# Tiles of their own for the retention's two outputs, beside a shared pool of nine slots

## The chip, the cores and the metric

One core of a Trainium2 chip runs the whole program. It has a matrix engine (PE in the profile, with its weight loads shown apart as PEld), a vector engine (DVE), a scalar engine (ACT), a GpSimd engine (POOL) and a queue that issues most transfers (SP). Each engine takes its own instructions strictly in the order in which they were placed at build time and stops at one whose inputs or whose memory are not free yet. The metric is the device time of one execution in microseconds, lower is better; the median of three runs is given.

## The reference

Two decoder layers on a sequence of 512 positions with 1024 channels, all in float32. A layer has three token mixers that share one input projection, a gated sum of their outputs, and a gated MLP:

```python
for l in range(DEPTH):                        # 2
    h = rmsnorm(x, norm_mix_g[l])
    proj = h @ w_in[l]                        # split into the pieces below
    # differential attention: 4 heads of 2 x 64, v of 128, blocks of 128 queries
    a = softmax(q1 @ k1 + bias) - lam * softmax(q2 @ k2 + bias)
    o_da = rmsnorm(a @ v, da_subln_g[l]) * (1.0 - lam_init)
    # retention: 4 heads of 64, chunks of 128, with rotary embedding
    o_ret = rmsnorm(retention(rq, rk, rv), ret_norm_g[l]) * silu(r_g)
    o_sc = sc_b * causal_dwconv(sc_c * sc_x, sc_conv_w[l], sc_conv_b[l])
    gates = sigmoid(gate_pre + b_gate[l])     # 3 x 1024
    y = (gates[0] * (o_da @ w_branch_da[l]) + gates[1] * (o_ret @ w_branch_ret[l])
         + gates[2] * (o_sc @ w_branch_sc[l]))
    x = x + y @ w_out[l]
    h = rmsnorm(x, norm_ffn_g[l])
    g_ff, u_ff = split(h @ w_ffn_in[l])       # 2 x 2816
    x = x + (silu(causal_dwconv(g_ff, ...)) * u_ff) @ w_ffn_out[l]
```

## The kernel before, in words

**Arithmetic.** Every float32 matrix product is made of three products in a faster format. An operand is split into a rounded part `hi` (a cast on ACT, line 150, 166 or 169) and the rest `lo` (a subtraction on DVE, line 151, 167 or 170), and `mm3` (lines 159 to 161) adds hi·hi, hi·lo and lo·hi. Weights are loaded by SP (line 137) into two raw slots and split into a ring of three `hi` and three `lo` tiles. A split activation is a pair of 128x512 tiles, that is 4 KB on each of the 128 partitions.

**The shared pool "N".** `pairN` and `wide` hand out tiles of 4 KB per partition with the tag N, of which there are nine (`NN = 9`). In the mixers of one layer these tiles live there: the retention's values `rv` (two), its gate `sg`, its natural keys `knh` and `knl`, its transposed queries and keys `rT` (four), and its outputs `omr0` and `omr1`; the short convolution's outputs `oms0` and `oms1`; and for each attention head h the projected queries and keys `nath`, the values `vh`, the transposed pair `qh` and `kh`, and the output `omh`. Later `y` and the MLP's `act` tiles follow. A new tile takes the slot of one whose last reader is done; until then its first writer waits.

**Order of the work.** The program text weaves two streams (`weave`): the first is the chain of small steps of the retention and of the four attention heads, the second (`filler`) the large projections. `filler` runs head 0's projection (PSUM tiles `pnh0`), the short convolution's first half, head 1's, its second half, head 2's, five steps of the short convolution's branch (`side(2)`), head 3's projection, and then the rest of `side(2)` and `side(1)`, the retention's branch. A piece of a side is a gate projection of 24 products 128x512 (`ptg16` to `ptg23` for side 2, `ptg8` to `ptg15` for side 1), followed by a branch projection of 6 (`pb02` to `pb72` and `pb01` to `pb71`; the first digit is the column block, the second the branch). At build time a scheduler with a timing model of its own then places the instructions of all streams on each engine, and gives out the slots in the order in which its model sees them free. So the size of a pool decides not only waits but the order itself.

**Where a head's projection ends.** `natural` fills all four PSUM banks of the pool `pm` ("main") with one head, 128 positions each. `evacuate` (lines 430 to 435) empties a bank in five steps: `nat` (ACT, 432), a square in place (ACT, 433), the split of the values into `v` (ACT, 169 and DVE, 170) and a sum of the squares into `msqk` (DVE, 435). Only when the last of these is done may the next user of the bank, for head 3 `pb22`, write there.

**The attention of a head** (lines 529 to 539) runs four query blocks i: scores `pS0hi` and `pS1hi` on PE (487, 488), bias and minimum on DVE (492), exponential on ACT (493), a combination on DVE (501 to 504), transposes `pThi` on PE (511), a split into `aThi` (ACT 166, DVE 167), products with the values into `po0h` or `po2h` on PE (523, 524), and `oh` (ACT 525, DVE 526). At the end `oh` is scaled (544), transposed into `ptoh` (284) and split into `omh` (169, 170).

**Two memory regions that alternate.** The layer's mixers have a pool `mp` on the right side of SBUF, and the MLP a pool there too, one after the other, over the same addresses. By the shapes in the program `mp` holds 55 KB per partition and the MLP's 64 KB.

Of the kernel before, what the change touches and what calls it, by code (L numbers as in the profile page):

```python
# [12 lines left out]
F32R = mybir.dt.float32r  # L13
# [7 lines left out]
P = 128  # L21
D = 1024
S = 512
# [25 lines left out]
G_MIX, G_FFN, B_GATE, G_Q, G_K, G_SUB, G_RET = 0, 8, 16, 40, 41, 42, 43  # L49
# [4 lines left out]
def trunk(ctx, tc, xT, wr, wh, wt, wda, wret, wsc, wo, wf, w2, par, lamp, relb, onehot, mask, rope, gtab, out):  # L54
# [20 lines left out]
    def pairN(name):  # L75
        return tp.tile([P, 2, S], F32R, tag="N", name=name, bufs=NN)
# [42 lines left out]
    def main(name):  # L119
        return pm.tile([P, S], F32, tag="main", name=name)  # L120
# [42 lines left out]
    def split(src, hi, lo, g=None):  # L163

        if g is None:
            A.copy(hi, src)
            V.tensor_tensor(lo, src, hi.bitcast(F32), ALU.subtract)
        else:
            A.activation(hi, src, AF.Copy, scale=g)
            V.scalar_tensor_tensor(lo, src, g, hi.bitcast(F32), ALU.mult, ALU.subtract)  # L170
        return hi, lo

    def split2(src, t, g=None):
        n = src.shape[-1]
        return split(src, t[:, 0, :n], t[:, 1, :n], g)
# [12 lines left out]
    ps = pa.tile([P, S], F32, tag="aux", name="ps_warm")  # L188
# [82 lines left out]
    def rms_cols(sq, n, scale, name):  # L271

        ms = small(n, f"ms{name}")
        V.tensor_reduce(ms, sq, AX.X, ALU.add)
        V.tensor_scalar(ms, ms, scale, EPS, ALU.mult, ALU.add)
        f = small(n, f"f{name}")
        rsqrt(f, ms, n, name)
        return f

    def transposes(src, name):  # L280

        ps = aux(name)
        for st in range(ST):
            T.transpose(ps[:, st * P : (st + 1) * P], src(st), ident)
        return ps
# [13 lines left out]
    def mix(l, mp):  # L299
        pt = pars[l]  # L300
        L = f"L{l}"
# [147 lines left out]
        om = [None] * KT  # L449
# [109 lines left out]
        def retention(p):  # L559
# [4 lines left out]
            for c in (p, 2 + p):  # L564
                ps = transposes(lambda st: rr[st][:, c * P : (c + 1) * P], f"ptr{c}{L}")
# [70 lines left out]
            f = rms_cols(sqv, 8, 1.0 / 64, f"r{p}{L}")  # L636
# [6 lines left out]
            yield  # L643
            yield
            ps = transposes(lambda st: o[:, st * P : (st + 1) * P], f"ptor{p}{L}")
            om[4 + p] = split2(ps, pairN(f"omr{p}{L}"), pt[:, G_RET : G_RET + 1])
            yield


# [75 lines left out]

        rest = filler()
        weave(staggered([(4 * p, retention(p)) for p in range(2)] + [(6 + 8 * h, attention(h)) for h in range(H)]), rest)

        y = []
# [5 lines left out]
        for e in range(KT):  # L735
            w = weights(wo[l, e], f"o{L}{e}")
            ps = main(f"po{e}{L}")
# [237 lines left out]
```

## Time and profile before

| | us |
|---|---|
| median of 3 runs (lowest, highest) | 1548.77 (1547.65, 1552.67) |
| the profiled execution, its own time | 1550.88 |
| its span from the first to the last instruction | 1549.1 |
| PE busy, PEld busy | 1526.5, 1345.9 |
| DVE busy, ACT busy | 1101.2, 731.9 |
| mean granted TensorE clock | 0.993 |

The profiled execution took 1550.88 us, of which 1.8 lie outside the span. A row of the timeline gives start, duration, engine, line, operation and tiles; brackets at its end give idle time of the engine just before it and what ended that. Layer numbers and buffer numbers are left out of names, so `v3L` is head 3's value tile in either layer, once in the first half of the span and once in the second. Where a matmul starts before the one ahead of it is shown to end, the two overlap in the engine's pipeline: the spacing of starts, not the duration, is what a matmul costs.

### The profile page before, as it was taken

To read this page: it belongs to the slowest core of one execution; us is meant where nothing else is said; L and a number is where in the kernel's file an instruction comes from. 1 tells how busy PE (TensorE), PEld (TensorE's weight loads), DVE (VectorE), ACT (ScalarE), POOL (GpSimd) and SP (SyncE) were. 2 spreads that over 40 slices of the span, in tenths; PEclk is the share of its full clock that TensorE was granted. 3 is DMA by queue.
4 is the path that set the end of the run, shared out by engine and by line. 5 is a ranking of instruction groups with operands and counts; after the bars stand their busy time and mean duration, and the time that the engine had idled before them with its cause. 6 is when DMAs were issued, how large, how long until landed. Compare 5 with 4: busy or idle time off the path is not lost.

```text
span 1549.1 us, 21866 instructions
## 1 busy us (share of the span) xinstructions
PE 1526.5 (99%) x8510; PEld 1345.9 (87%) x8510; DVE 1101.2 (71%) x2040; ACT 731.9 (47%) x1304; POOL 14.1 (1%) x27
## 2 busy tenths in 40 slices
PE   9999989999999999999999999899999999999998
PEld 7899878888887999899789999688888879988997
DVE  7588776655569996597666887665546789957963
ACT  4456555433344564365425565453334446634641
POOL 1000000000000000000100000000000000000000
PEclk9999999999999999999999999899999999999999
DMA  5322222232221332331322222222323132224213
GB/s 188 116 103 63 88 74 84 85 98 96 98 88 55 142 110 69 136 137 55 129 82 92 72 89 72 68 81 90 102 76 123 68 110 110 92 84 165 96 45 106
DMA packets 43287, 148.54 MB, mean 96 GB/s; under 512 B 5703, under 2 KB 6102, under 8 KB 37552
## 3 DMA queue, kind: packets, MB, share of 16 engines
q1 hardware_dynamic: 41328, 143.37, 27.7%
q0 software_dynamic: 1856, 3.77, 0.7%
q8 instruction: 67, 1.10, 0.3%
q14 instruction: 36, 0.29, 0.1%
HBM read 145.01 MB, written 3.42 MB: 96 GB/s over the span
## 4 chain that ended last, share of the span: by engine, by line
PE 92%; DVE 3%; DMA 2%; ACT 2%; issue 1%; SPq 0%; ACTq 0%; DVEq 0%
PE pnrvgL L161 1%; PE pnrvgL L159 1%; PE pnrvgL L160 1%; PE pnrqkL L160 1%; PE pnrqkL L161 1%; PE pnrqkL L159 1%; PE pnh2L L161 1%; PE pnh2L L160 1%; PE pnh2L L159 1%; PE pnh1L L161 1%; PE pnh1L L160 1%; PE pnh1L L159 1%; PE pnh0L L160 1%; PE pnh0L L159 1%; PE pnh0L L161 1%
## 5 line engine op out<-in xcount | busy, mean ns | idle before, releaser
L150 ACT CAST hi_tL<-raw_tL 128x1024 fp32r<-128x1024 f32 x60 | 62.9, 1049 | 135.0 <-DMA raw_tL<-in_wt 18.3
L150 ACT CAST hi_w2L<-raw_w2L 128x640 fp32r<-128x640 f32 (+2 forms) x64 | 49.4, 781 | 97.8 <-DMA raw_w2L<-in_w 49.8
L151 DVE TENSOR_TENSOR lo_tL<-raw_tL,hi_tL 128x1024 fp32r<-128x1024 f32 x60 | 73.4, 1224 | 19.0 <-ACT hi_tL L150 18.8
L151 DVE TENSOR_TENSOR lo_w2L<-raw_w2L,hi_w2L 128x640 fp32r<-128x640 f32 (+2 forms) x64 | 56.2, 889 | 37.8 <-ACT hi_w2L L150 35.7
L150 ACT CAST hi_fbL<-raw_fL 128x1024 fp32r<-128x1024 f32 x34 | 35.7, 1051 | 26.2 <-PE p216L L160 11.7
L150 ACT CAST hi_oL<-raw_oL 128x1024 fp32r<-128x1024 f32 x16 | 16.9, 1054 | 58.1 <-issue 19.5
L151 DVE TENSOR_TENSOR lo_fbL<-raw_fL,hi_fbL 128x1024 fp32r<-128x1024 f32 x34 | 41.6, 1222 | 1.7 <-ACT hi_fbL L150 1.6
L150 ACT CAST hi_faL<-raw_fL 128x512 fp32r<-128x512 f32 x34 | 21.1, 622 | 30.9 <-DMA raw_fL<-in_wf 26.8
L151 DVE TENSOR_TENSOR lo_fuL<-raw_fL,hi_fuL 128x1024 fp32r<-128x1024 f32 x10 | 12.2, 1224 | 19.6 <-ACT hi_fuL L150 19.6
L150 ACT CAST hi_fuL<-raw_fL 128x1024 fp32r<-128x1024 f32 x10 | 10.5, 1051 | 31.2 <-PE pg0L L160 11.0
L151 DVE TENSOR_TENSOR lo_faL<-raw_fL,hi_faL 128x512 fp32r<-128x512 f32 x34 | 23.4, 689 | 0.3
L150 ACT CAST hi_nrvgL<-raw_nrvgL 128x1024 fp32r<-128x1024 f32 x8 | 8.4, 1051 | 31.5 <-PE pnrvgL L161 13.5
L150 ACT CAST hi_fgL<-raw_fL 128x1024 fp32r<-128x1024 f32 x10 | 10.5, 1054 | 24.1 <-issue 9.5
L151 DVE TENSOR_TENSOR lo_oL<-raw_oL,hi_oL 128x1024 fp32r<-128x1024 f32 x16 | 19.6, 1224 | 2.8 <-ACT hi_oL L150 2.8
L151 DVE TENSOR_TENSOR lo_nrvgL<-raw_nrvgL,hi_nrvgL 128x1024 fp32r<-128x1024 f32 x8 | 9.8, 1224 | 12.6 <-ACT hi_nrvgL L150 12.6
L151 DVE TENSOR_TENSOR lo_nh0L<-raw_nh0L,hi_nh0L 128x768 fp32r<-128x768 f32 x8 | 7.7, 958 | 13.4 <-ACT hi_nh0L L150 13.4
L150 ACT CAST hi_nrqkL<-raw_nrqkL 128x1024 fp32r<-128x1024 f32 (+1 forms) x9 | 8.6, 953 | 16.1 <-issue 11.1
L150 ACT CAST hi_bdL<-raw_bdL 128x512 fp32r<-128x512 f32 x16 | 9.9, 618 | 10.7 <-PE pb50L L160 2.2
L151 DVE TENSOR_TENSOR lo_nrqkL<-raw_nrqkL,hi_nrqkL 128x1024 fp32r<-128x1024 f32 (+1 forms) x9 | 9.9, 1105 | 7.0 <-ACT hi_nrqkL L150 7.0
L150 ACT CAST hi_nh0L<-raw_nh0L 128x768 fp32r<-128x768 f32 x8 | 6.7, 838 | 15.4 <-PE pnh0L L161 7.8
L151 DVE TENSOR_TENSOR lo_fgL<-raw_fL,hi_fgL 128x1024 fp32r<-128x1024 f32 x10 | 12.2, 1222 | 2.1 <-ACT hi_fgL L150 2.1
L150 ACT CAST hi_nh3L<-raw_nh3L 128x768 fp32r<-128x768 f32 x8 | 6.7, 835 | 14.0 <-PE ptg17L L160 7.3
(8455 smaller groups left out, 5985.4 us busy)
## 6 DMA issues: line engine op xcount, KB each, us to landing
raw_fL<-in_wf SPq DMA_DIRECT2D x44, 1024.0 KB, 4.8
raw_tL<-in_wt SPq DMA_DIRECT2D x60, 512.0 KB, 3.3
raw_w2L<-in_w SPq DMA_DIRECT2D x32, 320.0 KB, 2.9
raw_oL<-in_wo SPq DMA_DIRECT2D x16, 512.0 KB, 3.3
raw_w2L<-in_w SPq DMA_DIRECT2D x16, 512.0 KB, 3.5
raw_nrvgL<-in_wr SPq DMA_DIRECT2D x8, 512.0 KB, 3.2
raw_bdL<-in_wda SPq DMA_DIRECT2D x16, 256.0 KB, 2.6
raw_w2L<-in_w SPq DMA_DIRECT2D x16, 256.0 KB, 2.6
```

Source lines behind the costliest of these rows:

```text
L150: A.copy(h, raw)
L151: V.tensor_tensor(w, raw, h.bitcast(F32), ALU.subtract)
L159: T.matmul(o, a[0], b[0], start=start, stop=False, skip_group_check=more)
L160: T.matmul(o, a[0], b[1], start=False, stop=False, skip_group_check=more)
L161: T.matmul(o, a[1], b[0], start=False, stop=stop, skip_group_check=more)
```

## The change

In `retention`, the output of head pair p is split into a tile of its own in the mixers' pool `mp`, with a name of its own and one buffer, and no longer into a slot of the tag N. Its shape, its writers and its readers (`side(1)`) stay. The nine N slots are left to the others; `mp` grows by two tiles of 4 KB to 63 KB per partition.

```diff
@@ -643,7 +643,7 @@
             yield
             yield
             ps = transposes(lambda st: o[:, st * P : (st + 1) * P], f"ptor{p}{L}")
-            om[4 + p] = split2(ps, pairN(f"omr{p}{L}"), pt[:, G_RET : G_RET + 1])
+            om[4 + p] = split2(ps, mp.tile([P, 2, S], F32R, name=f"omr{p}{L}"), pt[:, G_RET : G_RET + 1])
             yield
```

No instruction is added or taken away; the order moves on PE, DVE and ACT inside the mixers of both layers, and on SP and POOL it is the same. Two places show it, both in layer 0 where head 3's projection ends; layer 1 has the same moves.

On ACT, with the engines that a row waits for in brackets. Before, the rows from head 3's last square on: `o2`, `s022` to `s123` and `aT21` belong to head 2's attention, `v3` is the evacuation of head 3's values.

```order
L433 ACTIVATE pnh3L_2044<-pnh3L_2044 128x256
L525 COPY o2L_2020<-po02L_2192 128x128 [waits PE_49]
L527 ACTIVATE po02L_2192,mso2L_2022<-o2L_2020,zs2L_2021 128x128 [waits DVE_49]
L493 ACTIVATE s022L_2263,z22L_2256<-s022L_2263,mn022L_2264 128x384 [waits DVE_49]
L493 ACTIVATE s122L_2267,z22L_2256<-s122L_2267,mn122L_2268 128x384 [waits DVE_49]
L166 CAST aT21L_2274<-pT21L_2271 128x256 [waits PE_49]
L493 ACTIVATE s023L_2361,z23L_2354<-s023L_2361,mn023L_2362 128x512 [waits DVE_49]
L525 COPY o2L_2020<-po02L_2192 128x128 [waits PE_49,Activation_49]
L169 ACTIVATE v3L_2039<-pnh3L_2041,rmL_298 128x128 [waits PE_49]
L169 ACTIVATE v3L_2039<-pnh3L_2042,rmL_298 128x128
L169 ACTIVATE v3L_2039<-pnh3L_2043,rmL_298 128x128
L169 ACTIVATE v3L_2039<-pnh3L_2044,rmL_298 128x128
```

And now, from head 3's first bank on:

```order
L432 COPY nat3L_2038<-pnh3L_2041 128x256 [waits PE_49]
L433 ACTIVATE pnh3L_2041<-pnh3L_2041 128x256
L432 COPY nat3L_2038<-pnh3L_2042 128x256 [waits PE_49]
L433 ACTIVATE pnh3L_2042<-pnh3L_2042 128x256
L169 ACTIVATE v3L_2039<-pnh3L_2041,rmL_298 128x128 [waits Activation_49]
L166 CAST aT20L_2154<-pT20L_2152 128x128 [waits PE_49]
L169 ACTIVATE v3L_2039<-pnh3L_2042,rmL_298 128x128 [waits Activation_49]
L432 COPY nat3L_2038<-pnh3L_2043 128x256 [waits PE_49]
L433 ACTIVATE pnh3L_2043<-pnh3L_2043 128x256
L169 ACTIVATE v3L_2039<-pnh3L_2043,rmL_298 128x128 [waits Activation_49]
```

The four `v3` rows stood behind seven rows of head 2's attention and waited for PE; now each follows the square of its own bank, ahead of all those rows, and waits only for ACT itself.

On PE at the same place, before: the last products of head 3's projection, and behind them head 2's attention.

```order
L161 MATMUL pnh3L_2044<-hi_nh3L_2200,xs7mL_233 128x384
L511 MATMUL pT20L_2152<-ident,s020L_2030 128x128
L523 MATMUL po02L_2192<-v2L_1562,aT20L_2154 128x256
L524 MATMUL po02L_2192<-v2L_1562,aT20L_2154 128x128
L284 MATMUL pto1L_2248<-ident,o1L_1543 128x128 x4
L487 MATMUL pS022L_2257<-k2L_1934,q2L_1933 128x384
L488 MATMUL pS022L_2257<-klzL_122,q2L_1933 128x384
L487 MATMUL pS122L_2258<-k2L_1934,q2L_1933 128x384
```

And now (`pT20` stands eleven rows ahead of the first of these, among the products of `pnh3`):

```order
L161 MATMUL pnh3L_2044<-hi_nh3L_2200,xs7mL_233 128x384
L523 MATMUL po02L_2192<-v2L_1562,aT20L_2154 128x256
L159 MATMUL pb22L_2300<-oms0L_1034,hi_b2L_2296 128x512
L160 MATMUL pb22L_2300<-oms0L_1034,hi_b2L_2296 128x512
L161 MATMUL pb22L_2300<-oms0L_1034,lo_b2L_2297 128x512
L159 MATMUL pb22L_2300<-oms1L_1517,hi_b2L_2296 128x512
L160 MATMUL pb22L_2300<-oms1L_1517,hi_b2L_2296 128x512
L161 MATMUL pb22L_2300<-oms1L_1517,lo_b2L_2297 128x512
L524 MATMUL po02L_2192<-v2L_1562,aT20L_2154 128x128
L159 MATMUL ptg19L_2327<-xs0mL_139,hi_tL_2323 128x512
```

Eighteen rows of head 2's attention stood between head 3's projection and `pb22`; now one row does, and `pto1` and the scores `pS022` follow after `pb22`, `ptg19`, `pb32` and seven products of `ptg20`. From `ptg11` on (side 1) both orders run alike again.

## The prediction

> **What bounds the kernel now.** I read the page first, then PE's waits, then windows around the longest of them.
>
> ```profile
> span 1549.1 us, 21866 instructions
> ...
> PE 1526.5 (99%) x8510; PEld 1345.9 (87%) x8510; DVE 1101.2 (71%) x2040; ACT 731.9 (47%) x1304; POOL 14.1 (1%) x27
> ...
> PE 92%; DVE 3%; DMA 2%; ACT 2%; issue 1%; SPq 0%; ACTq 0%; DVEq 0%
> ```
>
> PE is the bound nearly everywhere: 99% busy, 92% of the chain of waits. The change alters no product, so it can only return time in which PE stands or runs slowly. PE's waits, longest in total first:
>
> ```profile
> PE po02L L523 <- ACT aT20L L166: 3.9, 2, 2.0
> PE pto1L L284 <- DVE o1L L544: 2.7, 2, 1.4
> PE pb22L L159 <- DVE msqk3L L435: 2.2, 2, 1.4
> ...
> PE po02L L524 <- DVE aT20L L167: 1.4, 2, 0.7
> ```
>
> These four come twice each, once a layer, and lie side by side: 10.2 of PE's 22.6 us idle. The windows around them (length, then busy time and count of PE, PEld, DVE, ACT, POOL; then the granted clock):
>
> ```profile
> 150.00:170.00 20.00, 20.00 (x116) 18.70 (x115) 16.30 (x55) 15.59 (x41) 0.00 (x0) 1.00 0.30 102
> 196.00:206.20 10.20, 10.20 (x66) 10.15 (x65) 7.72 (x22) 8.33 (x23) 0.00 (x0) 1.00 0.28 86
> 206.20:219.00 12.80, 6.73 (x26) 3.99 (x24) 8.95 (x35) 7.39 (x25) 0.00 (x0) 0.87 0.19 56
> 219.00:229.00 10.00, 10.00 (x44) 8.29 (x45) 9.59 (x31) 3.73 (x9) 0.00 (x0) 1.00 0.00 0
> 971.20:984.00 12.80, 8.03 (x25) 5.14 (x23) 9.00 (x35) 7.39 (x25) 0.00 (x0) 0.67 0.15 56
> 984.00:989.20 5.20, 5.17 (x12) 4.11 (x13) 5.10 (x18) 1.44 (x5) 0.00 (x0) 0.51 0.00 0
> ```
>
> PE is full before and after, and in 12.8 us per layer it issues some 25 matmuls where it issued 66 in the 10.2 us ahead. The reason is in the timeline, ACT and PE rows:
>
> ```profile
> 203.89 0.37 ACT L432 COPY nat3L<-pnh3L 128x256 f32<-128x256 f32 x1
> 216.55 0.40 PE L488 MATMUL pS123L<-klzL,q2L 128*128 128x512 f32 x1
> 217.32 1.14 ACT L169 ACTIVATE v3L<-pnh3L,rmL 128x128 fp32r<-128x128 f32 x4
> 218.34 0.71 ACT L169 ACTIVATE om1L<-pto1L,par 128x512 fp32r<-128x512 f32 x1
> 219.00 0.50 PE L159 MATMUL pb22L<-oms0L,hi_b2L 128*128 128x512 f32 x1 [1.44 <-DVE msqk3L L435]
> ```
>
> `nat3` empties head 3's banks from 203.89 on, yet `v3`, from the same banks, starts only at 217.32. What ended at 216.95 is `pS123`, the last reader of `q2` and `k2`: two N slots fell free, `v3` and `om1` took them at once, and 1.7 us later `pb22` got its bank. A count of the nine slots at 205 us agrees: `omr0`, `omr1`, `oms0`, `oms1`, `om0`, `v2`, `q2`, `k2`, `nat3`. All four main banks were thus held for a slot, and PE had only head 2's attention, a chain of short steps through DVE and ACT. The two tiles that the change moves sit in that count for all of it:
>
> ```profile
> L169 ACT ACTIVATE omr0L<-ptor0L,par x2: 687/687/687, 114.0 to 879.0; 128x512 fp32r<-128x512 f32 x2
> L161 PE MATMUL pb71L<-omr0L,lo_b1L x2: 389/389/389, 318.1 to 1085.5; 128*128 128x512 f32 x2
> ```
>
> From 114.0 to 318.1 us (879.0 to 1085.5 in layer 1) `omr0` keeps a slot.
>
> **The change part by part.** It adds and removes no instruction. What the stall costs is the time of the stretch less what its work costs at full pace. The stretch runs from `pT20` to `pb22`:
>
> ```profile
> 206.19 0.27 PE L511 MATMUL pT20L<-ident,s020L 128*128 128x128 f32 x1
> ...
> 971.15 0.27 PE L511 MATMUL pT20L<-ident,s020L 128*128 128x128 f32 x1
> ...
> 984.03 0.79 PE L159 MATMUL pb22L<-oms0L,hi_b2L 128*128 128x512 f32 x1 [0.75 <-DVE msqk3L L435]
> ...
> 989.24 0.39 PE L159 MATMUL ptg19L<-xs2mL,hi_tL 128*128 128x512 f32 x1
> ```
>
> That is 219.00 - 206.19 = 12.81 us in layer 0 and 984.03 - 971.15 = 12.88 in layer 1. Full pace, by starts of neighbours:
>
> ```profile
> 205.84 0.33 PE L160 MATMUL pnh3L<-lo_nh3L,xs7mL 128*128 128x384 f32 x1
> 206.01 0.34 PE L161 MATMUL pnh3L<-hi_nh3L,xs7mL 128*128 128x384 f32 x1
> ...
> 201.38 0.34 PE L523 MATMUL po21L<-v1L,aT13L 128*128 128x256 f32 x1
> 201.55 0.22 PE L524 MATMUL po21L<-v1L,aT13L 128*128 128x128 f32 x1
> 201.61 0.33 PE L523 MATMUL po21L<-v1L,aT13L 128*128 128x256 f32 x1
> ...
> 220.49 0.39 PE L159 MATMUL ptg19L<-xs0mL,hi_tL 128*128 128x512 f32 x1
> 220.72 0.39 PE L160 MATMUL ptg19L<-xs0mL,hi_tL 128*128 128x512 f32 x1
> ...
> 301.65 0.44 PE pto3L L284 x4
> ```
>
> So 0.17 us for 384 columns, 0.23 for 512, 0.23 for a pair of `po`, 0.11 for a transpose. The stretch holds 10 transposes (1.10), 3 pairs (0.69), 4 of 384 (0.68) and 4 of 512 (0.92): 3.4 us. It could give back 12.81 - 3.4 = 9.4 and 12.88 - 3.4 = 9.5 us. In layer 1 the clock stays low after it (0.51): the 12 matmuls from 984.03 to 989.24 take 5.21 where 12 x 0.23 = 2.76 is full pace, 2.4 more. Together 21.3.
>
> PE's busy time would give less: idle of 12.80 - 6.73 and 12.80 - 8.03, 10.8 us in all, since the thinly spaced matmuls count as busy for their whole latency. I take the starts, because they are what the next matmul waits for. [...]
>
> Is the stall gone? In the changed order `v3` waits for no slot, its rows stand right behind the squares, and `pb22` comes one row behind `pnh3`. How such an end looks without the stall, head 2 shows, whose end at 159 us needs the same steps:
>
> ```profile
> 159.12 0.35 ACT L432 COPY nat2L<-pnh2L 128x256 f32<-128x256 f32 x1
> ...
> 161.23 0.63 ACT L169 ACTIVATE v2L<-pnh2L,rmL 128x128 fp32r<-128x128 f32 x2
> ```
>
> There `v2` follows `nat2` after 2.1 us and PE is busy all 20.00 us of 150 to 170. The one row now ahead of `pb22` is the first `po02`, which needs `aT20`; its wait of 2.0 us stood behind `pT20` directly, and now eleven products of 384 (1.9 us) lie between. `pto1` moves behind 43 products of 512 (`pb22`, `ptg19`, `pb32` and seven of `ptg20`). I leave 0.5 us per layer, 1.0 in all, for waits that the new order makes; the bounds are 0 (as head 2's end) and all of the waits for `aT20` and `o1`, 3.9 + 1.4 + 2.7 = 8.0. A gain beyond the stall is excluded: PE is full on both sides.
>
> **Moved rows elsewhere** I cost at nothing. Where `v1`, `v2`, `om0` and `aT10` change places (115 to 190 us), PE has no wait, its cover is the stream of `ptsc` and `pnh` products; if that were lost, such a wait costs what `aT20`'s does, 2 us. SP and POOL keep their orders. In layer 1 the wait for the MLP's region moves from `bias`'s transfer to `qz1`'s memset one row ahead on POOL, with that transfer and `lam`'s queued behind:
>
> ```profile
> 741.98 0.95 POOL L312 MEMSET qz1L<- 128x1024 f32 x1
> 742.89 0.76 POOL L317 DMA_DIRECT2D biasL<-skew  x1
> ...
> L571 DVE CAST qz1L<-rT0L x4: 407/419/425, 60.3 to 829.6; 64x512 fp32r<-64x512 f32 x4
> ```
>
> The transfer started without a wait at 742.89, so the region was free; and `qz1` is first written by DVE at 829.6, 87 us of cover.
>
> **Sum.** 21.3 - 1.0 = 20.3 us. The profiled execution took 1550.88, so 1530.6; the median of the runs stands 2.1 lower, so **1528.5 us**. Its own range: all 21.3 back, less 1.1 of scatter (median to lowest run), 1526.4; with all 8.0 of new waits 1548.8 - 13.3 = 1535.5.
>
> The low clock is the least certain term. The same stall left layer 0 at 1.00 from 219 on and layer 1 at 0.51 for 5.2 us. [...]
>
> **The rivals.**
>
> *DVE takes PE's place* (chance 0.13). DVE has 8.95 + 9.59 = 18.5 us of work from 206.2 to 229, in which PE's own work is 3.4 + 10.0 = 13.4. If PE had to follow DVE there, the 22.8 us shrink to 18.5 and no further: 4.3 a layer, with the clock's 2.4 it is 11.0, **1537.8**. For it: DVE is at 96% from 219 to 229. Against: PE is full in that window all the same, and the pieces pulled in (`ptg`, `pb`) need less of DVE than the evacuation.
>
> *Only the bank's wait goes* (0.07). If the attention's chain still stopped PE as before, because rows behind `po02` cannot pass it, the wait booked on `msqk3` (2.2) and the clock's 2.4 return: **1544.2**. For it: the waits on `aT20` and `o1` are larger and name no slot. Against: `pb22` to `ptg20` now stand ahead of `pto1`.
>
> *Nothing* (0.03): another holder, a raw or `hi` slot, keeps `pb22` back as long: **1548.8**. Against: the changed `v3` rows carry no wait but ACT's.
>
> *Weights run late* (0.05, slower). In the stall the loader got ahead; without it every gate tile is wanted 9.4 us earlier.
>
> ```profile
> L150 ACT CAST hi_tL<-raw_tL 128x1024 fp32r<-128x1024 f32 x60 | 62.9, 1049 | 135.0 <-DMA raw_tL<-in_wt 18.3
> ...
> L151 DVE TENSOR_TENSOR lo_tL<-raw_tL,hi_tL 128x1024 fp32r<-128x1024 f32 x60 | 73.4, 1224 | 19.0 <-ACT hi_tL L150 18.8
> ...
> 225.91 1.06 ACT L150 CAST hi_tL<-raw_tL 128x1024 fp32r<-128x1024 f32 x1 [5.41 <-PE ptg19L L160]
> ```
>
> A tile that is not ready shows its cast and subtraction, 1.05 + 1.22 = 2.3 us. From `ptg19` on there are 13 gate tiles a layer, 26 in all; 21.3 / 2.3, from the tenth late tile on, it is slower than before. With half of them late in both layers, 13 x 2.3 = 30 us: **1557**. For it: casts waited 18.3 us for `raw_t` in all. Against: at 225.91 the cast waits 5.41 us for PE to release a tile, so the ring is ahead; and SP's order is the same.
>
> **How the numbers follow.** The forecast has 0.72, the rivals the rest. A run of this kernel tells about 0.3% (4.6 us, 1544.1) from no change. Faster: the forecast, the first rival and half the second, 0.72 + 0.13 + 0.03 = 0.88; within: the other half and *nothing*, 0.07; slower 0.05. The range reaches from the forecast's low end, a little scatter added, to just past the first rival: 1525.5 to 1539.
>
> **What would show it.** Right: `v3` starts within 3 us of `nat3` in both layers; the wait of `pb22` on `msqk3` is gone; PE's idle time falls from 22.6 to 12 or 13; no window past 110 us in the mixers under a clock of 0.95; `pb22` starts within 1 us of `pnh3`'s last product. Wrong: new PE waits on `aT20`, `o1` or `lo_t` above 2 us a layer, or a stall in 115 to 190 us where there was none.

## The result, and the profile after

The changed kernel takes **1526.94 us** (median; 1525.99 to 1526.99), the kernel before 1550.24 beside it: ratio 0.9848, 95% interval 0.983 to 0.9867. A second measurement, with another five runs, gave 1527.34 and 0.9855 (0.9839 to 0.987). Forecast were 1528.5 us and a range of 1525.5 to 1539. The saving is 23.3 us by the medians and 1549.1 - 1525.2 = 23.9 by the profiled spans, where the sum said 20.3.

The page of the changed kernel, the lines that answer to those of before:

```profile
span 1525.2 us, 21885 instructions
PE 1514.3 (99%) x8510; PEld 1340.4 (88%) x8510; DVE 1100.5 (72%) x2040; ACT 732.6 (48%) x1304; POOL 14.1 (1%) x27
PE 95%; DVE 3%; DMA 2%; ACT 1%; issue 0%; SPq 0%; ACTq 0%; DVEq 0%
```

PE now stands idle for 10.9 us, where it was 22.6. All its waits above 0.5 us (total, times, longest):

```profile
PE p204L L159 <- ACT hi_w2L L150: 1.6, 2, 0.8
PE por00L L617 <- ACT PT00L L166: 1.6, 1, 1.6
PE ps_warm L190 <- POOL ones L184: 1.1, 1, 1.1
PE p223L L161 <- DVE lo_w2L L151: 1.0, 2, 0.5
PE pnrqkL L159 <- ACT hi_nrqkL L150: 0.7, 1, 0.7
```

The four waits of the stall (`po02` twice, `pto1`, `pb22`) are gone, and no wait on `aT20`, `o1` or `msqk3` has come in their place. The windows of the stall, with the same bounds as before (length, busy time and count of PE, PEld, DVE, ACT, POOL; then granted clock):

```profile
206.20:219.00 12.80, 12.80 (x61) 10.69 (x60) 11.40 (x38) 4.85 (x11) 0.00 (x0) 1.00 0.34 102
219.00:229.00 10.00, 10.00 (x54) 8.49 (x53) 6.30 (x16) 5.20 (x13) 0.00 (x0) 1.00 0.09 27
971.20:984.00 12.80, 12.80 (x67) 10.77 (x66) 9.04 (x22) 6.00 (x16) 0.00 (x0) 1.00 0.19 63
984.00:989.20 5.20, 5.20 (x30) 4.46 (x29) 4.76 (x7) 5.12 (x9) 0.00 (x0) 1.00 0.06 13
```

PE is full in all of them and its clock is 1.00 throughout; it issues 61 and 67 matmuls where it issued 26 and 25. The end of head 3's projection in the timeline, layer 0 and then layer 1:

```profile
201.12 0.36 ACT L432 COPY nat3L<-pnh3L 128x256 f32<-128x256 f32 x1
202.50 0.36 ACT L169 ACTIVATE v3L<-pnh3L,rmL 128x128 fp32r<-128x128 f32 x1
203.75 0.33 PE L161 MATMUL pnh3L<-hi_nh3L,xs7mL 128*128 128x384 f32 x1
203.92 0.28 PE L523 MATMUL po02L<-v2L,aT20L 128*128 128x256 f32 x1
204.04 0.40 PE L159 MATMUL pb22L<-oms0L,hi_b2L 128*128 128x512 f32 x1
...
956.28 0.36 ACT L432 COPY nat3L<-pnh3L 128x256 f32<-128x256 f32 x1
957.79 0.36 ACT L169 ACTIVATE v3L<-pnh3L,rmL 128x128 fp32r<-128x128 f32 x1
959.04 0.33 PE L161 MATMUL pnh3L<-hi_nh3L,xs7mL 128*128 128x384 f32 x1
959.33 0.40 PE L159 MATMUL pb22L<-oms0L,hi_b2L 128*128 128x512 f32 x1
```

`v3` follows `nat3` after 1.4 and 1.5 us (13.4 before), and `pb22` starts 0.29 us behind the last product of head 3, in both layers.

**Where the 23.9 us lie.** I measured the piece of each layer that holds the stall from the first product of `pnh3` to that of `ptg7` (side 1), since both orders are alike behind `ptg11` (from `pb31` on, and not from `ptg11`'s start). Before:

```profile
184.37 0.33 PE L159 MATMUL pnh3L<-hi_nh3L,xs0mL 128*128 128x384 f32 x1
376.10 0.39 PE L159 MATMUL ptg7L<-xs0mL,hi_tL 128*128 128x512 f32 x1
949.33 0.33 PE L159 MATMUL pnh3L<-hi_nh3L,xs0mL 128*128 128x384 f32 x1
1143.48 0.39 PE L159 MATMUL ptg7L<-xs0mL,hi_tL 128*128 128x512 f32 x1
```

After:

```profile
182.51 0.33 PE L159 MATMUL pnh3L<-hi_nh3L,xs0mL 128*128 128x384 f32 x1
364.27 0.39 PE L159 MATMUL ptg7L<-xs0mL,hi_tL 128*128 128x512 f32 x1
937.80 0.33 PE L159 MATMUL pnh3L<-hi_nh3L,xs0mL 128*128 128x384 f32 x1
1119.57 0.39 PE L159 MATMUL ptg7L<-xs0mL,hi_tL 128*128 128x512 f32 x1
```

The piece fell from 191.73 to 181.76 us in layer 0 and from 194.15 to 181.77 in layer 1: 10.0 and 12.4. In front of it, rows that moved out of it add 0.4 a layer (`pnh2` to `pnh3` is 44.4 us instead of 44.0), so the change is worth 9.6 + 12.0 = 21.6 us in these two profiles. The other 2.3 us come earlier, before any moved row. Window 75 to 90 us, before and then after:

```profile
75.00:90.00 15.00, 13.18 (x69) 11.54 (x69) 14.24 (x42) 9.56 (x24) 0.80 (x1) 0.89 0.40 135
```

```profile
75.00:90.00 15.00, 13.78 (x77) 12.01 (x78) 14.52 (x41) 8.97 (x22) 0.80 (x1) 1.00 0.44 148
```

Both hold the wait at `por00` (1.8 and 1.6 us), but in the profile of before the clock fell to 0.89 behind it, and 69 matmuls were issued instead of 77. That is 1.8 us up to the first product of `ptsc20` (1.6 behind the wait and 0.2 in it), and 0.4 lies in the start-up.

### The profile page after: what moved, and what is told of

Same layout as the page of the kernel before. It is cut to its first block, busy times and chain, and to the rows that moved or that the text cites. A ratio compares the mean times of both kernels' runs of the same rounds, so it can differ in the third digit from the quotient of the medians.

```text
span 1525.2 us, 21885 instructions
## 1 busy us (share of the span) xinstructions
PE 1514.3 (99%) x8510; PEld 1340.4 (88%) x8510; DVE 1100.5 (72%) x2040; ACT 732.6 (48%) x1304; POOL 14.1 (1%) x27
## 4 chain that ended last, share of the span: by engine, by line
PE 95%; DVE 3%; DMA 2%; ACT 1%; issue 0%; SPq 0%; ACTq 0%; DVEq 0%
PE pnrvgL L161 1%; PE pnrvgL L159 1%; PE pnrvgL L160 1%; PE pnrqkL L160 1%; PE pnrqkL L161 1%; PE pnrqkL L159 1%; PE pnh2L L161 1%; PE pnh2L L159 1%; PE pnh1L L161 1%; PE pnh3L L161 1%; PE pnh3L L160 1%; PE pnh2L L160 1%; PE pnh3L L159 1%; PE pnh1L L160 1%; PE pnh1L L159 1%; PE pnh0L L159 1%
## 5 line engine op out<-in xcount | busy, mean ns | idle before, releaser
L150 ACT CAST hi_w2L<-raw_w2L 128x640 fp32r<-128x640 f32 (+2 forms) x64 | 49.4, 781 | 97.9 <-DMA raw_w2L<-in_w 55.1
L151 DVE TENSOR_TENSOR lo_tL<-raw_tL,hi_tL 128x1024 fp32r<-128x1024 f32 x60 | 73.4, 1223 | 19.4 <-ACT hi_tL L150 19.1
L150 ACT CAST hi_nrvgL<-raw_nrvgL 128x1024 fp32r<-128x1024 f32 x8 | 8.4, 1053 | 31.2 <-PE pnrvgL L161 13.5
L151 DVE TENSOR_TENSOR lo_nh0L<-raw_nh0L,hi_nh0L 128x768 fp32r<-128x768 f32 x8 | 7.6, 956 | 13.6 <-ACT hi_nh0L L150 13.6
L150 ACT CAST hi_nh2L<-raw_nh2L 128x768 fp32r<-128x768 f32 x8 | 6.7, 840 | 11.9 <-PE ptsc21L L160 9.2
```

Of the source, the lines that this page charges most:

```text
L150: A.copy(h, raw)
L151: V.tensor_tensor(w, raw, h.bitcast(F32), ALU.subtract)
```

## The experiments

Theory: `v3` cannot empty the four main banks for want of a slot, and PE waits for a bank; who holds the slots does not matter. Its rivals: it is the layout or omr's own place; it is `om1`, the other tile that took a slot behind `pS123`; it is both. All medians but that of the first measurement stand beside further runs of the kernel before (medians 1549.97, 1550.76 and 1550.53 us). The "piece" is that from `pnh3` to `ptg7`, layer 0 / layer 1.

| kernel | median us | ratio (95%) | piece, us | mean clock |
|---|---|---|---|---|
| before | 1550.0 to 1550.8 | 1 | 191.7 / 194.2 | 0.9926 |
| the change | 1526.9, 1527.3 | 0.985 | 181.8 / 181.8 | 1.000 |
| room only | 1549.91 | 1.0003 (0.9991 to 1.0016) | 191.6 / 192.6 | 0.9933 |
| omr0 alone | 1527.91 | 0.9858 (0.9837 to 0.988) | 182.0 / 182.0 | 1.000 |
| oms instead | 1527.17 | 0.9852 (0.9831 to 0.9873) | 181.8 / 181.8 | 1.000 |
| v3 alone | 1530.88 | 0.9876 (0.9854 to 0.9897) | 183.5 / 183.6 | 1.000 |
| om1 alone | 1546.15 | 0.9971 (0.9961 to 0.9981) | 192.1 / 190.4 | 0.9961 |
| two slots held | 1551.98 | 1.0009 (0.9995 to 1.0023) | 194.2 / 193.9 | 0.9917 |
| fill, 8 products | 1548.34 | 0.9986 (0.9975 to 0.9998) | 190.9 / 194.4 | 0.9939 |
| fill, 8 + 5 | 1538.97 | 0.9927 (0.9912 to 0.9943) | 188.4 / 189.9 | 0.9994 |
| one more step | 1528.66 | 0.986 (0.9844 to 0.9876) | 180.2 / 180.2 | 1.000 |

**The room without the move.**

```diff
         bias_t = mp.tile([P, H, S], F32, name=f"bias{L}")
+        room = [mp.tile([P, 2, S], F32R, name=f"room{p}{L}") for p in range(2)]
```

> The kernel before with the mixers' region made as large as in the change (two 4 KB tiles that nobody writes or reads stand in it), but omr0 and omr1 still in the nine shared slots. If the slots are the cause: as before, 1548 to 1553 us, the stall of some 12.8 us a layer between pT20 and pb22 there, v3 some 13 us behind nat3, PE idle 22 us. If it is where the region and its tiles lie: about 1527.

Nothing changes: 1.0003. The region is as large as in the change, the instructions stand in the order of before on every engine, and the stall is there. It also settles the difference at 75 to 90 us. The same window of this kernel:

```profile
75.00:90.00 15.00, 12.93 (x74) 11.26 (x74) 14.52 (x42) 9.83 (x24) 0.80 (x1) 1.00 0.40 132
```

With the order of before and a longer wait at `por00` (2.1 us) the clock stayed at 1.00. No row has moved yet in this window, so the low clock there was a draw in the profile of before; the run further down that holds two slots has it too (0.89), with the change's tiles.

**One slot instead of two.**

```diff
-            om[4 + p] = split2(ps, pairN(f"omr{p}{L}"), pt[:, G_RET : G_RET + 1])
+            om[4 + p] = split2(ps, mp.tile([P, 2, S], F32R, name=f"omr0{L}") if p == 0 else pairN(f"omr1{L}"), pt[:, G_RET : G_RET + 1])
```

> Only omr0 gets a tile of its own; omr1 stays in the nine slots. If what counts is that v3 finds one slot when head 3's banks are ready: nearly all comes back, 1526 to 1530 us, v3 within 3 us of nat3; om1, which then is the one without a slot, waits in an auxiliary bank that nobody needs. If both tiles of the pair v3 and om1 have to find a slot: about half of 21.5 us is left, 1537 to 1541, with a new PE wait behind om1.

1527.91 us: one slot does it. The second tile that wanted one is now `om1`, which is written 13 us later than in the change (214.57 there):

```profile
L169 ACT ACTIVATE om1L<-pto1L,par x1: 692/692/692, 227.9 to 227.9; 128x512 fp32r<-128x512 f32 x1
```

PE has no wait from it, and the piece is 182.0 us against 181.8. `omr1`'s 4 KB buy nothing that can be measured.

**Another pair.**

```diff
-            om[6 + j] = split2(y, pairN(f"oms{j}{L}"))
+            om[6 + j] = split2(y, mp.tile([P, 2, S], F32R, name=f"oms{j}{L}"))
```

> Another pair is moved: oms0 and oms1 (the short convolution's outputs) get tiles of their own in the mixers' pool, omr0 and omr1 stay in the slots. If it is the count of nine at 205 us: as the change, 1525 to 1529 us. If it is something of omr itself (when it is written, who reads it): as before, 1548 to 1553.

1527.17 us, and the piece is the same to 0.01 us. Nothing is special about omr; that any other tile of the count would have done as well is likely, but only this pair was tried.

**Only the tile that waits.**

```diff
-            v = pairN(f"v{h}{L}")
+            v = mp.tile([P, 2, S], F32R, name=f"v3{L}") if h == 3 else pairN(f"v{h}{L}")
```

> Nothing that holds a slot is moved; only the tile that waits, v3, gets 4 KB of its own in the mixers' pool, once a layer. The nine slots stay full until pS123. If v3's evacuation of the four main banks is what stopped PE: 1526 to 1531 us, pb22 within 1 us of pnh3's last product, om1 still behind pS123. If om1 or the full slots as such are the cause: 1544 to 1553.

1530.88 us. The slots stay full, `om1` comes at 229.4 us, behind `pS123`, and yet 19 of the 23 us are back: it is `v3`. The rest, 1.7 us a layer, lies in part at the end of the projection. This kernel's PE timeline there:

```profile
203.96 0.27 PE L511 MATMUL pT20L<-ident,s020L 128*128 128x128 f32 x1
204.32 0.47 PE L159 MATMUL pb22L<-oms0L,hi_b2L 128*128 128x512 f32 x1
...
205.54 0.39 PE L161 MATMUL pb22L<-oms1L,lo_b2L 128*128 128x512 f32 x1
206.35 0.47 PE L159 MATMUL ptg19L<-xs0mL,hi_tL 128*128 128x512 f32 x1 [0.42 <-DVE fo1L L239]
```

`ptg19` starts 0.81 us behind `pb22`'s last product, where 0.23 is full pace, and waits 0.42 of it for DVE; `pb22` starts 0.36 us behind `pT20`, where 0.11 is. These two gaps are 0.8 of the 1.7 us. Another 0.4 is no loss: as in the kernel before, `pnh2` to `pnh3` takes 44.0 us here and 44.4 in the change, so that work only stands inside the piece. The other 0.5 was not traced; the rows stand in another order here than in the change.

**Only the other tile.**

```diff
-            om[h] = split2(ps, pairN(f"om{h}{L}"), pt[:, G_SUB : G_SUB + 1])
+            om[h] = split2(ps, mp.tile([P, 2, S], F32R, name=f"om1{L}") if h == 1 else pairN(f"om{h}{L}"), pt[:, G_SUB : G_SUB + 1])
```

> The counterpart of the run in which v3 alone got a tile: now om1, the other tile that took a slot after pS123, gets 4 KB of its own in the mixers' pool, once a layer; v3 stays in the nine slots. If v3 on the main banks is the cause: v3 still starts behind pS123, some 13 us after nat3, and the time is as before, 1546 to 1552 us. If om1's bank counted too: some 5 to 10 us of the 23 come back, 1540 to 1545.

1546.15 us, at the low edge of the first theory and above the second. Its timeline has the stall, with `v3` released by `pS123`:

```profile
201.86 0.37 ACT L432 COPY nat3L<-pnh3L 128x256 f32<-128x256 f32 x1
213.56 0.63 PE L487 MATMUL pS123L<-k2L,q2L 128*128 128x512 f32 x1
214.23 1.14 ACT L169 ACTIVATE v3L<-pnh3L,rmL 128x128 fp32r<-128x128 f32 x4 [0.80 <-PE pS123L L487]
215.81 0.77 PE L159 MATMUL pb22L<-oms0L,hi_b2L 128*128 128x512 f32 x1
```

This row names what before only the times suggested: ACT waits for `pS123`, the last reader of `q2` and `k2`. It waits 0.80 us only. The rest of the delay shows as ACT's order, in which `v3` stands behind head 2's rows; in the kernel before ACT comes to `v3` at 217.32, when `pS123` has been done since 216.95. So the full pool shows mostly in where the scheduler put `v3`, and little as a wait. Order and wait come from the same slots and were not taken apart. `v3` comes 12.4 us behind `nat3` instead of 13.4, and the mean clock is 0.9961 instead of 0.9926; by the line between clock and span further down, that is worth 3.3 of the 4.6 us gained. Why the clock is better here was not pursued.

**The slots taken away again.**

```diff
             om[4 + p] = split2(ps, mp.tile([P, 2, S], F32R, name=f"omr{p}{L}"), pt[:, G_RET : G_RET + 1])
+            if p < 2:
+                hold.append(pairN(f"hold{p}{L}"))
+                V.tensor_copy(hold[p][:, 0, 0:4], om[4 + p][0][:, 0:4].bitcast(F32))
...
+        hold = []
...
             yield from side(1, wret, lambda: om[4:6])
+            for t in hold:
+                h = small(16, f"h{L}")[:, 0:4]
+                V.tensor_copy(h, t[:, 0, 0:4].bitcast(F32))
```

> The changed kernel with two slots taken away again: omr0 and omr1 have their own tiles, but at the place where each is written a tile is taken from the nine slots, 128x4 numbers are copied into it, and they are read (into a scratch tile) after the last product of branch 1. Four more DVE instructions of some 0.1 us a layer. If the slots that are held are the cause, wherever omr lies: the stall is back in both layers, 1547 to 1553 us. If it is the two tiles' own place: 1527.

1551.98 us: omr has its own tiles as in the change, and all of the gain is gone, since two slots are held. In the timeline `v3` and `om1` start together again, 13.5 us behind `nat3`:

```profile
204.21 0.37 ACT L432 COPY nat3L<-pnh3L 128x256 f32<-128x256 f32 x1
217.66 1.14 ACT L169 ACTIVATE v3L<-pnh3L,rmL 128x128 fp32r<-128x128 f32 x4
218.68 0.71 ACT L169 ACTIVATE om1L<-pto1L,par 128x512 fp32r<-128x512 f32 x1
```

PE's order is that of the kernel before again, up to `ptg21` behind the stall. With the room run, this shows it from both sides: the place of omr does nothing, and the slots held bring order and stall back.

**The change again, and one step more for retention.** The second kernel tries for a version that beats both, at the wait of `por00`.

> The changed kernel once more, beside the next run: 1526 to 1528 us, clock 1.00 in all runs; its wait at por00 (1.6 us) is there again. If the 1.9 us that the first profiles differ at 75 to 90 us were due to the change, they return here against the kernel before of the same call; if they were a draw of the clock, the time to ptsc20 differs from the room run's by 1 us or less.

```diff
             scores(1)
             yield
+            if p == 0:
+                yield
             values(0)
```

> The changed kernel with one more step given to the other work before the first head pair's retention values (p = 0): the products of por00 stand later, so PT00 should be ready. If the order simply moves: the wait of 1.6 us at por00 is gone and nothing else comes, 1525 to 1526 us. If everything behind retention shifts by a step and finds other waits: 1527 to 1530.

The change gave 1527.34 us. Its time to `ptsc20` was 83.6 us against 84.9 in the room run, 1.3 apart and not 1 or less; 0.9 of that is the start-up, which ends at 55.1 and 56.0 us. With one more step the wait at `por00` is gone, but `ptr1` waits 1.0 us for DVE instead and `pnh3` starts later. In its profile `ptg7` still comes 0.5 us sooner in layer 0 than in the first profile of the change (363.73 against 364.27); in layer 1 it is 1.0 late, behind a wait of 1.2 us at `pb5` in layer 0's MLP. The median is 1528.66, which gains nothing.

**Is the clock part of the stall?** The kernel before spread over 1546.3 to 1554.8 us, the changed one, in nine runs, over 1526.0 to 1529.9. Each run has its span and its granted clock: over 49 runs of the kernel before, clocks of 0.989 to 0.998, a straight line gives span = 1541.5 + 955 x (1 - clock), with a correlation of -0.92. In 21 runs of the four kernels without the stall (the change, omr0, oms, v3) the clock was 0.999 or 1.000. By the line the median span of 1548.4 us holds 6.9 us of low clock; it is drawn on from 0.998, the highest clock seen, to 1. The profile of before shows where the low clock lies:

```profile
77.78:81.18 3.40, 3.40 (x15) 3.01 (x13) 3.34 (x9) 3.35 (x10) 0.00 (x0) 0.50 0.83 320
210.90:214.30 3.40, 3.03 (x11) 2.20 (x11) 1.34 (x5) 0.82 (x5) 0.00 (x0) 0.50 0.12 45
975.50:989.10 13.60, 12.16 (x33) 8.78 (x34) 10.20 (x35) 6.12 (x20) 0.00 (x0) 0.50 0.05 19
```

The clock is at half (0.50) in these three stretches and full (1.00) elsewhere: 3.4 us behind `por00`, 3.4 in layer 0's stall, 13.6 in layer 1's. Half of 20.4 us is 10.2, and 1 - 10.2 / 1549.1 is the 0.993 of the whole. The first stretch is not the stall's, so the stall need not account for all of the line's 6.9 us. To see whether idle time brings it, products were put into the stall that keep PE busy and do nothing else.

```diff
-                    st_[0]["po"] = aux(f"po{i}{h}{L}").rearrange("p (i a e) -> p i a e", i=2, a=2)
+                    pof = aux(f"po{i}{h}{L}")
+                    if h == 2 and i == 0:
+                        for _ in range(8):
+                            T.matmul(pof, kh2[:, 0, 0:P], qs2[:, 0], start=True, stop=True)
+                    st_[0]["po"] = pof.rearrange("p (i a e) -> p i a e", i=2, a=2)
```

> The kernel before with its stall left as it is, and eight products of 512 columns added in it (q2 by k2, written to po02's bank and overwritten by the first real product there; the result is not used), right behind pT20, where PE waits 2.0 us for aT20: 8 x 0.23 = 1.84 us, so the chain of the stall should stay as long. If the clock falls because PE stands idle in the stall: mean clock above the 0.9927 of the kernel before, towards 0.997, and 2 to 5 us faster, 1545 to 1548 us, though no stall is removed. If the clock is independent of the idle time: 1549 to 1552, or later by what the products add.

The second one adds, in `transposes` for `pto1` alone:

```diff
         ps = aux(name)
+        for _ in range(fill):
+            T.matmul(ps[:, :P], ones, ones, start=True, stop=True)
```

> As the run before, and five more products of 128x128 ahead of the four transposes of pto1, in its bank, where PE waits 1.4 us for o1; their results are not used either. By the idle time: the clock closer to 1.00 still, 1543 to 1547 us. By a clock independent of it: 1549 to 1553.

With the eight products PE's order is otherwise that of before until behind `pb22`; a few rows of ACT and DVE change places. More work made the kernel 2.2 us faster, with an interval (0.9975 to 0.9998) that only just leaves out no change, and the clock rose from 0.9923 beside it to 0.9939: the sign that was expected, less of it than expected, and a median of 1548.34 between the two ranges. The profile of that kernel does not show the gain. PE's wait for `aT20` is down to 0.3 us, but its clock in the stall, layer 0 and layer 1, is no better than the 0.87 and 0.67 of before:

```profile
204.31 2.09 PE L520 MATMUL po02L<-q2L,k2L 128*128 128x512 f32 x8
...
206.00:219.00 13.00, 9.14 (x37) 6.17 (x36) 10.33 (x35) 7.21 (x25) 0.00 (x0) 0.87 0.09 23
971.00:984.00 13.00, 10.75 (x30) 7.61 (x31) 9.38 (x32) 6.41 (x21) 0.00 (x0) 0.54 0.08 21
```

With eight and five the clock is 0.9994 and the time 1538.97, below both ranges, though `v3` is still held back. The stall's windows and its start:

```profile
206.00:219.00 13.00, 10.96 (x59) 8.44 (x58) 12.32 (x45) 7.00 (x24) 0.00 (x0) 1.00 0.08 21
971.00:984.00 13.00, 11.54 (x47) 8.98 (x46) 10.03 (x39) 5.59 (x17) 0.00 (x0) 0.87 0.01 2
...
201.88 0.37 ACT L434 COPY nat3L<-pnh3L 128x256 f32<-128x256 f32 x1
211.40 1.14 ACT L169 ACTIVATE v3L<-pnh3L,rmL 128x128 fp32r<-128x128 f32 x4
```

This run is not clean as to time: the added products let scores of head 2 stand ahead of `pto1`, and the stall itself is shorter (`v3` 9.5 us behind `nat3` instead of 13.4). At a clock of 1.000 its runs span 1536.4 to 1537.2 us, 4 to 5 below the line's 1541.5; by the line, that much is the order, and the other 6 to 7 of its 11.6 us the clock. So nearly all of the clock can come back while `v3` is still held for 9.5 us, and with PE busier than before. That the added work alone did it is not shown, since the order and the length of the stall changed with it.

## Why the prediction was right, and where its sum was off

- **The cause** held. Slots full (two slots held: 1551.98), `v3` the one that matters (v3 alone: 1530.88), `pS123` the one that ends its wait (om1 alone, in the row's own words), omr only one holder among others (oms: 1527.17). The prediction speaks of a wait for a slot; in the trace most of the delay shows as ACT's order, which comes back with the slots held. What it left open was whether both moved tiles were needed: one is enough.
- **The two stretches.** 9.4 and 9.5 + 2.4 us were costed; the two profiles show 9.6 and 12.0. The measure by starts was right. PE's idle time alone would have given 10.8, the time without a weight load (12.80 - 3.99 and 12.80 - 5.14) 16.5.
- **The term that was mis-sized** is the 1.0 us left for waits that the new order makes. It measured 0: no wait on `aT20` or `o1` is on the list, and the products that moved between each pair covered them. PE's idle time came out at 10.9 us and not at 12 or 13. Without the four waits it would be 22.6 - 10.2 = 12.4; the rest went with smaller waits that the prediction did not count, on `aT21` in the stall (0.5), at `pnrqk` (0.6) and at `por00` (0.2). The low end of the forecast (all 21.3 back, less the scatter: 1526.4) was the better value.
- **Some luck is in the number.** The forecast started from a median of 1548.77; with one more run the kernel before has 1550.24. The saving was 3.0 us more than the sum, the time only 1.6 us less than the forecast.
- **The clock.** Booked were 2.4 us, as the least certain term. The 49 runs put 6.9 us of the median's 23 on it; most of the rest stood inside the two stretches, which ran at 0.87 and 0.67 in that profile. So the sum held, but only for a run with a clock like that one (0.993). Against the run before with the highest clock (0.998, span 1544.5) the saving is 19.3 us, against the one with the lowest (0.989, 1553.0) 27.8. By the line the low clock is 6.9 of 1548.4 us, 0.45%. What sets the length of the half-clock stretches (3.4, 3.4 and 13.6 us in the profile of before), and why the mean clock differs from run to run, no run shows.
- **2.3 us of the profiles' difference** were not in the sum and are not the change's: a draw of the clock at `por00` (1.6), as the room run shows, a wait there that was 0.2 longer, and the start-up (0.4).
- **Moved rows elsewhere** cost nothing, as said. The changed kernel from 90 to 196 us:

```profile
90.00:196.00 106.00, 106.00 (x604) 97.82 (x603) 87.12 (x242) 65.14 (x145) 0.00 (x0) 1.00 0.24 79
```

- **DVE in PE's place** did not come. DVE has 11.40 + 6.30 = 17.7 us of work in the 22.8 us in which PE is now full; PE waits for none of it. **Only the bank's wait** and **nothing** are out with the four waits gone. **Weights late** is out too: in the groups of the changed kernel the subtraction of a weight tile waits as before (19.4 us in all, 19.0 before), and no product of a gate waits for one.

```profile
L151 DVE TENSOR_TENSOR lo_tL<-raw_tL,hi_tL 128x1024 fp32r<-128x1024 f32 x60 | 73.4, 1223 | 19.4 <-ACT hi_tL L150 19.1
```

## What to carry to other kernels

A pool of shared buffers can stop an engine that does not wait for it by name: here PE, by way of ACT and the banks. The list of waits named `aT20`, `o1` and `msqk3`, all of them victims; the cause was found by asking which tile is emptied late, counting the holders of its pool at that moment, and seeing what ended when it went on. Then one buffer less in the count was enough (`omr0` alone), and another pair held over the whole stall (`oms0` and `oms1`) did as well as omr.

Cost such a stall by the starts of the instructions and by the clock, not by idle time: two stretches with 10.8 us of idle time were worth 21.6.

## What was not expected of the hardware

Every run of a kernel with the whole stall lost clock, 0.998 at best, and over the 49 runs of the kernel before the lost clock goes with most of the spread: a thousandth of mean clock is about 1 us here. A stall of 12.8 us in which PE still issues 25 matmuls, and never waits longer than 2.0 us at a time, costs by the line at most some 3.5 us a layer that way (6.9 in all, the stretch behind `por00` counted in). That eight products which nobody reads made the kernel 2.2 us faster, and eight and five took the clock to 0.9994, points the same way; whether fewer would do, and where in the stall they must stand, was not tried. Without the stall the two layers run alike: 181.76 and 181.77 us for the same piece.
